# A hybrid mLSTM and stick-breaking layer on one core: every k turned by VectorE and DRAM, with the projections put in another order

## The chip, the core and the metric

The kernel runs on one core of a Trainium2 chip. A core has TensorE (PE: matmuls and their weight loads), VectorE (DVE), ScalarE (ACT), GpSimd (POOL) and SyncE (SP), which issues most DMAs. Each engine works through its own instructions in order and waits at semaphores for the others. The metric is the device time of one execution in microseconds. Names of engines and line numbers are those of the profile.

## What is computed

One layer on x of 512 tokens by 1024 channels, all in float32. The part that the change touches is stick-breaking attention: 8 heads of 128 channels, in two sets of four ("first" and "second" below), each with its own q, k, V and gate z, which are slices of one input projection.

```python
h = rmsnorm(x, norm_w)
proj = jnp.einsum('bsd,de->bse', h, w_in) + b_in
(mq, mk, mv, mi, mf, mo, mz, sq, sk, sv, sz, gates) = jnp.split(proj, split_at, axis=-1)
...
qs = rmsnorm(to_heads(sq, SB_HEADS), sb_q_norm_w)
ks_ = rmsnorm(to_heads(sk, SB_HEADS), sb_k_norm_w)
os_ = stick_breaking_attention(qs, ks_, to_heads(sv, SB_HEADS))
y_s = os_.transpose(0, 2, 1, 3).reshape(b_, s_, SB_WIDTH) * jax.nn.silu(sz)

g_m, g_s = jnp.split(jax.nn.sigmoid(gates), N_BRANCH, axis=-1)
merged = (g_m * jnp.einsum('bse,ed->bsd', y_m, w_proj_m)
          + g_s * jnp.einsum('bse,ed->bsd', y_s, w_proj_s))
x = x + jnp.einsum('bsd,de->bse', merged, w_out)
```

The other branch, an mLSTM (mq to mz, four heads of 256), runs behind the attention and is not changed.

## The kernel before

Every float32 product is made of three matmuls: both operands are split into a high and a low part (`split`, L99 to L101: ACT copies the high part, DVE subtracts it to get the low one), and high by high, high by low and low by high are added in PSUM (`mm3`, L95 to L97).

The projections are cut into units. A unit is one slice of weights (512 KB) with 24 matmuls of 512 columns. A loop over c runs them in order. In iteration c the kernel writes, in this order: the evacuation of unit c - 1 from PSUM; whatever was put down for c in `later` (`defer(n, fn)` puts it n units ahead, `at_unit(c, fn)` at a fixed place); the split of the weights of unit c + 2, and their loads up to unit c + 4 (`ahead`); the first half of unit c's matmuls; one step of each attention head that is running, and the first step of a head that begins; the second half of the matmuls. So each engine's order follows from the unit numbers. `by_dma` units have their low weights finished by a DMA that POOL issues and that adds (L127 to L129: two copies on ACT) and not by DVE.

Units of before: 0 to 3 first q; 4 to 7 half of the gates of the merge (GS), a filler while operands for the pairs are made; 8 to 21 and 22 to 35 two pairs; 36 to 39 first z; 40 to 43 second q; 44 to 47 second k; 48 to 51 second z; 52 to 55 half of GM, the other gates; then the mLSTM's. E is 36. A pair makes two projections together from 14 units of 12 matmuls each, by sums of weights (X, Y, V, Z) and of operands (`form`). The first pair is second V with the mLSTM's V, both parked in DRAM (`v_park`, L1060). The second is first V with first k. A pair's evacuation (`Pair.add`, L1040) adds the bias row on DVE; then a DMA from POOL (L1043) adds a part that ACT copied out earlier.

k and q come out with tokens on partitions. `norm` (L405) makes the sums of squares on ACT, four per 128 tokens; for k DVE scales the rows (L420). The scores need channels on partitions. `TURNED` lists which are turned without PE, two heads at a time (g 0 is heads 0 and 1, g 1 heads 2 and 3): `turn` (L432) transposes blocks of 32 by 32 on DVE into `ty`, `move` stores them to DRAM (`t_d`, four DMAs, L440), `back` loads them (`tz`, four DMAs, L445), and q's get their weight on DVE (L452). All of q is turned so, and k's g 1. k's g 0 is transposed by PE in the first step of its head (`head`, L482). That step also splits both operands (`qtt`, `ktt`). Step 1 makes the scores, steps 2 and 3 the products along the stick on DVE (L519 to L537); later steps turn the result through DRAM (`a_d`, `az`), split it (`ath`, `atl`) and multiply by V. First set's heads begin at units 37, 39, 42 and 44, second set's from unit 50 on. In a unit of `REST` no head steps.

Two pools of PSUM have four banks each: `dps` for units and a pair's bank "a", `aps` for attention and a pair's other banks. A unit of q or k by tokens needs four `dps` banks, two in each half of its first unit; a z or gate unit needs one.

Of the kernel before, what the change touches and what calls it, by code (L numbers as in the profile page):

```python
# [15 lines left out]
T = 512  # L16
# [22 lines left out]
def tile_hybrid_layer(  # L39
# [157 lines left out]
    later = {}  # L197
    now = [0]

    def by_plan(s, name, fn):  # L200
        if s:
            defer(1, fn)
        else:
            later.setdefault(E - 6, []).append(fn) if name == "q" else defer(2, fn)

    def defer(n, fn):
        later.setdefault(now[0] + n, []).append(fn)

# [150 lines left out]
    class SbSet:  # L359
# [5 lines left out]
            self.tz = {}  # L365
            self.count = {"q": 0, "k": 0, "v": 0}

        def z_group(self):
            def evac(ct, ps):
                sg = blk("tmp")  # L370
                b = bias(32 + 4 * self.s + ct)
                nc.scalar.activation(sg, ps, AF.Sigmoid, bias=b)
                t = blk("y", name="ys")
                nc.vector.scalar_tensor_tensor(t, ps, b, sg, op0=OP.add, op1=OP.mult)
                y_s[4 * self.s + ct] = t

            chan_group(w_in, C_SZ + 512 * self.s, 512, h_mov, evac)

# [19 lines left out]
        def norm(self, name, tb, t):  # L398
            self.raw[name][tb] = t
            ssq = tiny.tile([128, 4], F32, name="ssq", bufs=2)  # L400
            rr = tiny.tile([128, 8], F32, name="r" + name, bufs=8 if name == "q" else 4)
            r = rr[:, 0:4]
            junk = blk("om", BF, (128,), name="sqj")
            for h in range(4):
                nc.scalar.activation(junk, t[:, h * 128:(h + 1) * 128], AF.Square,  # L405
                                     accum_out=ssq[:, h:h + 1])
            rstd(r, ssq, 128, EPS)
            self.count[name] += 1
            last = self.count[name] == TB
            if name == "q":  # L410
                rn = rr[:, 4:8]
                nc.gpsimd.tensor_scalar(rn, r, -1.0, None, op0=OP.mult)
                self.r[tb] = (r, rn)
                if last:
                    by_plan(self.s, "q", lambda: self.turn(name, 0))
            else:
                def scale():
                    for h in range(4):
                        hs = slice(h * 128, (h + 1) * 128)
                        nc.vector.tensor_scalar(t[:, hs], t[:, hs], r[:, h:h + 1], None, op0=OP.mult)  # L420
                    if last:
                        done.add(("k", self.s))
                        by_plan(self.s, "k", lambda: self.turn(name, 1))
                defer(1, scale)

        def turn(self, name, g):

            ty = sp.tile([128, 8, TB, 32], F32, name="ty", tag="A", bufs=4)  # L430
            for tb in range(TB):
                nc.vector.transpose(ty[:, :, tb, :],  # L432
                                    self.raw[name][tb][:, 256 * g:256 * g + 256].rearrange("p (x j) -> p x j", j=32))

            def move():
                tz = blk("qk", F32, (2, 4, 128), name="tz")
                self.tz[name, g] = tz
                park = dp.tile([32, 2, 4, 4, 128], F32, name="t_d", tag="t_d", bufs=3)
                for a in range(4):
                    nc.sync.dma_start(park[:, :, :, a].rearrange("i h b x -> i (h b) x"),  # L440
                                      ty[32 * a:32 * a + 32].rearrange("i g n j -> i g (n j)"))

                def back():
                    for b in range(4):
                        nc.sync.dma_start(tz[32 * b:32 * b + 32].rearrange("i h a x -> i h (a x)"),  # L445
                                          park[:, :, b].rearrange("i h a x -> i h (a x)"))

                defer(2 if not self.s and name == "q" else 1, back)

            def weight():  # L450
                z = self.tz[name, g]
                nc.vector.tensor_scalar(z, z, qkw, None, op0=OP.mult)  # L452

            defer(1, move)
            if name == "q":
                defer(4 if self.s else 6, weight)
            if name == "q" and g == 0:
                defer(2, lambda: self.turn(name, 1))


        def v_parts(self, tb, t):
            vh = blk("vh", FR, (576,))[:, 0:512]
# [8 lines left out]
        def head(self, h):  # L471
            hs = slice(h * 128, (h + 1) * 128)
            tr = []
            for name in ("q", "k"):
                th, tl = own = two("qk", FR, name=name + "tt")
                if (name, self.s, h // 2) in TURNED:
                    tp = self.tz[name, h // 2][:, h % 2].rearrange("p a (i j) -> p i a j", j=32)
                    th, tl = [x.rearrange("p (i a j) -> p i a j", a=4, j=32) for x in own]
                else:
                    tp = att_ps()  # L480
                    for tb in range(TB):
                        nc.tensor.transpose(tp[:, tb * 128:(tb + 1) * 128], self.raw[name][tb][:, hs], ident)  # L482
                if name == "q" and not (name, self.s, h // 2) in TURNED:
                    nc.scalar.activation(th, tp, AF.Copy, scale=qkw)
                    nc.vector.scalar_tensor_tensor(tl, tp, qkw, th.bitcast(F32), op0=OP.mult, op1=OP.subtract)
                else:
                    split(tp, th, tl)
                tr.append(own)
            yield
            (qh, ql), (kh, kl) = tr  # L490
# [214 lines left out]
    class MPair:  # L705
# [11 lines left out]

            chan_group(w_in, C_MO + 512 * self.p, 512, h_mov, evac)

        def z_group(self):  # L720
            def evac(ct, ps):
                sg = blk("tmp")
                b = bias(24 + 4 * self.p + ct)
# [365 lines left out]
    for i in range(2):  # L1089
        at_unit(3, form_sum, 3, i)  # L1090

    for tb in range(TB):
# [480 lines left out]
```

## Time and profile before

| | us |
|---|---|
| median of 3 runs | 681.86 |
| the runs | 681.48, 681.86, 686.51 |
| the profiled execution | 686.68 |
| its span | 685.0 |
| DVE, busy | 497.3 |
| ACT, busy | 372.5 |
| POOL, busy | 114.9 |

The profile is of one execution, which took 1.7 us more than its span. Sums on its rows are compared with 686.68 first, and with the median after that. Unit 36 begins at 137.17 us, unit 37 at 142.61, unit 38 at 154.55, unit 45 at 199.00 and unit 46 at 207.79; units 47 and 48 begin at 214.49 and 219.94, unit 49 at 226.65. Matmul ends are modelled, so starts are the better guide: unit 36's 24 matmuls begin 0.227 us apart.

### The profile page before, as it was taken

To read this page: it belongs to the slowest core of one execution; us is meant where nothing else is said; L and a number is where in the kernel's file an instruction comes from. 1 tells how busy PE (TensorE), PEld (TensorE's weight loads), DVE (VectorE), ACT (ScalarE), POOL (GpSimd) and SP (SyncE) were. 2 spreads that over 40 slices of the span, in tenths; PEclk is the share of its full clock that TensorE was granted. 3 is DMA by queue.
4 is the path that set the end of the run, shared out by engine and by line. 5 is a ranking of instruction groups with operands and counts; after the bars stand their busy time and mean duration, and the time that the engine had idled before them with its cause. 6 is when DMAs were issued, how large, how long until landed. Compare 5 with 4: busy or idle time off the path is not lost.

```text
span 685.0 us, 9337 instructions
## 1 busy us (share of the span) xinstructions
PE 673.8 (98%) x3114; PEld 561.4 (82%) x3114; DVE 497.3 (73%) x852; ACT 372.5 (54%) x702; POOL 114.9 (17%) x265
## 2 busy tenths in 40 slices
PE   7999999989999999999999999999999999999998
PEld 5888888868888888888888888888888888888886
DVE  6777778756759878978888654569973466467997
ACT  6576545447586665654654646344455854234451
POOL 4023121412263222310011001110000120001020
PEclk9999999989999999999999999999999999999999
DMA  7566793965989866847458631435344468967333
GB/s 251 141 229 170 245 239 101 212 189 121 262 210 247 241 165 199 225 123 201 100 117 185 150 104 57 134 106 148 100 136 122 125 219 260 272 187 161 116 84 102
DMA packets 134464, 115.65 MB, mean 169 GB/s; under 512 B 17370, under 2 KB 105844, under 8 KB 134416
## 3 DMA queue, kind: packets, MB, share of 16 engines
q1 hardware_dynamic: 129232, 101.82, 51.1%
q0 software_dynamic: 5040, 13.11, 10.8%
q8 instruction: 24, 0.39, 0.2%
q14 instruction: 24, 0.20, 0.1%
q10 hardware_dynamic: 144, 0.13, 0.1%
HBM read 83.00 MB, written 18.93 MB: 149 GB/s over the span
## 4 chain that ended last, share of the span: by engine, by line
PE 91%; DMA 2%; DVE 2%; ACT 2%; issue 1%; POOL 1%; SPq 1%; DVEq 0%; ACTq 0%; POOLq 0%
PE dps L95 23%; PE dps L97 22%; PE dps L96 22%; PE dps L971 5%; PE aps L971 4%; PE aps L96 3%; PE aps L97 3%; PE aps L95 3%; DMA stg<-in_w_in_dram 2%; PE dps L1446 1%; PE dps L1448 1%; PE dps L1447 1%; ACT sqj L405 1%; PE aps L853 1%; PE aps L855 1%
## 5 line engine op out<-in xcount | busy, mean ns | idle before, releaser
L95 PE MATMUL dps<-hh,wh 128*128 128x512 f32 x448 | 176.4, 394 | 0.0
L97 PE MATMUL dps<-hh,wl 128*128 128x512 f32 x448 | 175.5, 392 | 0.0
L96 PE MATMUL dps<-hl,wh 128*128 128x512 f32 x448 | 175.4, 392 | 0.0
L101 DVE TENSOR_TENSOR wl<-stg,wh 128x1024 fp32r<-128x1024 f32 x73 | 89.2, 1222 | 69.5 <-ACT wh L100 68.8
L100 ACT ACTIVATE wh<-stg 128x1024 fp32r<-128x1024 f32 x73 | 76.7, 1052 | 42.9 <-PE dps L96 22.5
L97 PEld LDWEIGHTS dps<-hh,wl 128*128 128x128 f32 x448 | 84.7, 189 | 18.2
L96 PEld LDWEIGHTS dps<-hl,wh 128*128 128x128 f32 x448 | 84.8, 189 | 17.0
L95 PEld LDWEIGHTS dps<-hh,wh 128*128 128x128 f32 x448 | 84.9, 189 | 16.8
L743 ACT ACTIVATE tmp<-acc 128x512 f32<-128x512 f32 x16 | 10.1, 633 | 52.9 <-DVE acc L740 52.9
L95 PE MATMUL dps<-wh,hh 128*128 128x512 f32 x96 | 37.5, 391 | 0.0
L97 PE MATMUL dps<-wh,hl 128*128 128x512 f32 x96 | 37.4, 390 | 0.0
L96 PE MATMUL dps<-wl,hh 128*128 128x512 f32 x96 | 37.4, 390 | 0.0
L740 DVE SCALAR_TENSOR_TENSOR acc<-tmp,vec,acc 128x511 f32<-128x511 f32 (+2 forms) x48 | 36.0, 750 | 1.7
L519 DVE TENSOR_TENSOR_SCAN om<-om 128x512 f32<-128x512 f32 (+3 forms) x32 | 26.1, 816 | 0.0
L95 PE MATMUL dps<-yh,wh 128*128 128x512 f32 x64 | 24.9, 389 | 0.0
L96 PE MATMUL dps<-yl,wh 128*128 128x512 f32 x64 | 24.9, 389 | 0.0
L97 PE MATMUL dps<-yh,wl 128*128 128x512 f32 x64 | 24.9, 389 | 0.0
L129 POOL DMA_DIRECT2D wl<-stg x11 | 9.8, 888 | 89.6 <-DVE gback L1177 45.9
L507 ACT ACTIVATE om<-aps,rq 128x512 f32<-128x512 f32 (+3 forms) x32 | 16.7, 523 | 14.3 <-PE aps L97 14.3
L863 ACT ACTIVATE hns<-aps,hst 128x256 f32<-128x256 f32 x16 | 7.6, 475 | 28.2 <-DVE hst L862 21.1
L509 POOL TENSOR_SCALAR_AFFINE_SELECT om<-om 128x128 f32<-128x128 f32 x32 | 14.5, 452 | 44.5 <-ACT om L507 44.3
L101 DVE TENSOR_TENSOR atl<-az,ath 128x384 fp32r<-128x384 f32 (+1 forms) x24 | 13.8, 603 | 10.4 <-ACT ath L100 6.1
(303 smaller groups left out, 1533.9 us busy)
## 6 DMA issues: line engine op xcount, KB each, us to landing
stg<-in_w_in_dram SPq DMA_DIRECT2D x71, 512.0 KB, 4.8
wl<-stg POOLq DMA_DIRECT2D x11, 512.0 KB, 5.7
a_d<-ay SPq DMA_DIRECT2D x8, 640.0 KB
az<-a_d SPq DMA_DIRECT2D x32, 160.0 KB, 4.5
stg<-in_w_proj_s_dram SPq DMA_DIRECT2D x8, 512.0 KB
B<-in_w_out_dram SPq DMA_DIRECT2D x8, 512.0 KB, 8.3
stg<-in_w_proj_m_dram SPq DMA_DIRECT2D x8, 512.0 KB, 3.7
dst<-u POOLq DMA_DIRECT2D x12, 256.0 KB, 4.8
```

Of the source, the lines that this page charges most:

```text
L95: nc.tensor.matmul(ps, ah, bh, start=first, stop=False)
L96: nc.tensor.matmul(ps, ah, bl, start=False, stop=False)
L97: nc.tensor.matmul(ps, al, bh, start=False, stop=last)
L100: nc.scalar.activation(hi, src, AF.Copy)
L101: nc.vector.tensor_tensor(lo, src, hi.bitcast(F32), op=OP.subtract)
L129: nc.gpsimd.dma_start(out=self.wl, in_=self.st, accum_op=OP.add)
L507: nc.scalar.activation(om[:, 0:n], zp, AF.Sigmoid, scale=rn[:, h:h + 1])
L509: nc.gpsimd.affine_select(out=om[:, ts], in_=om[:, ts], compare_op=OP.is_gt, fill=1.0, base=0, channel_multiplier=1, pattern=[[-1, 128]])
L519: nc.vector.tensor_tensor_scan(back, back, back, 1.0, op0=OP.mult, op1=OP.bypass)
L740: nc.vector.scalar_tensor_tensor(acc[:, j:], t[:, 0:T - j], cw(3 - j, ch), acc[:, j:], op0=OP.mult, op1=OP.add)
L743: nc.scalar.activation(t, acc, AF.Sigmoid)
L971: nc.tensor.matmul(pr.bank[key, tb], a, w[:, i, :], start=begin and n == 0, stop=end and n == 2, skip_group_check=again)
```

## The change

No arithmetic changes. In the order of units, the filler 4 to 7 is first z, its result parked in DRAM (`z_park`) and loaded back in units 39 to 42 (`y_back`). The pair of first V and first k comes first (8 to 21), the pair of second V and the mLSTM's V next (22 to 35). Second q is 36 to 39, second k 40 to 43, second z 44 to 47, the half of GS that was the filler 48 to 51. The rest stays where it was.

All of k is turned by DVE and DRAM; `TURNED`, `by_plan` and PE's transposes go. For the first set q turns in units 9 and 13, k in 30 and 31 (`TURN`), and `tz` is loaded in units 33 and 37 for q, 34 and 38 for k (`TZ_BACK`). There `ty` lies in the buffers of tag qk, since the buffers A hold a pair's weights. For the second set, q and k turn one and two units behind their last norm. First heads begin at 36, 38, 41 and 44, and the first `REST` unit is 43 where it was 47. Weights finished by POOL's DMA are units 39 and 41 to 44, where they were 40 to 43 and 45 to 48.

```diff
-SB_START = [E + n for n in (1, 3, 6, 8, 14, 16, 18, 20)]
+SB_START = [E + n for n in (0, 2, 5, 8, 14, 16, 18, 20)]
-TURNED = {("q", 0, 0), ("q", 0, 1), ("q", 1, 0), ("q", 1, 1), ("k", 0, 1), ("k", 1, 1)}
-REST = {E + n for n in (11, 48)}
+TURN = {"q": (9, 13), "k": (30, 31)}
+TZ_BACK = {("q", 0): E - 3, ("q", 1): E + 1, ("k", 0): E - 2, ("k", 1): E + 2}
+REST = {E + n for n in (7, 48)}
...
-                t = blk("y", name="ys")
+                t = sg if dst is not None else blk("y", name="ys")
                 nc.vector.scalar_tensor_tensor(t, ps, b, sg, op0=OP.add, op1=OP.mult)
-                y_s[4 * self.s + ct] = t
+                if dst is None:
+                    y_s[4 * self.s + ct] = t
+                else:
+                    nc.sync.dma_start(dst[128 * ct:128 * ct + 128, :], t)
...
+        def turns(self, name):
+            for g in range(2):
+                if self.s:
+                    defer({"q": (1, 2), "k": (1, 2)}[name][g], lambda g=g: self.turn(name, g))
+                else:
+                    later.setdefault(TURN[name][g], []).append(lambda g=g: self.turn(name, g))
...
-                if (name, self.s, h // 2) in TURNED:
-                    tp = self.tz[name, h // 2][:, h % 2].rearrange("p a (i j) -> p i a j", j=32)
-                    th, tl = [x.rearrange("p (i a j) -> p i a j", a=4, j=32) for x in own]
-                else:
-                    tp = att_ps()
-                    for tb in range(TB):
-                        nc.tensor.transpose(tp[:, tb * 128:(tb + 1) * 128], self.raw[name][tb][:, hs], ident)
...
+                tp = self.tz[name, h // 2][:, h % 2].rearrange("p a (i j) -> p i a j", j=32)
+                th, tl = [x.rearrange("p (i a j) -> p i a j", a=4, j=32) for x in own]
+                split(tp, th, tl)
...
-        return lambda tb, t: defer(2 + tb % 2, lambda: sets[s].v_parts(tb, t))
+        return lambda tb, t: defer((2, 5)[tb % 2], lambda: sets[s].v_parts(tb, t))
...
-    chan_group(w_in, C_GS, 512, h_mov, park(gs_park, 48))
+    z_park = dp.tile([512, T], F32, name="z_park")
+    sets[0].z_group(z_park)
+    Pair(C_SV, C_SK, to_parts(0), to_norm(0, "k"))
     Pair(C_SV + 512, C_MV, to_dram(0), to_dram(1))
-    Pair(C_SV, C_SK, to_parts(0), to_norm(0, "k"))
...
+    for ct in range(4):
+        at_unit(E + 3 + ct, y_back, ct)
...
-    sets[0].z_group()
     sets[1].qk_group("q", C_SQ)
     sets[1].qk_group("k", C_SK)
     sets[1].z_group()
+    chan_group(w_in, C_GS, 512, h_mov, park(gs_park, 48))
...
-    for un in units[n_proj - 3:] + [units[E + n] for n in (4, 5, 6, 7, 9, 10, 11, 12)]:
+    for un in units[n_proj - 3:] + [units[E + n] for n in (3, 5, 6, 7, 8)]:
```

Line numbers of the changed kernel differ a little (L97 is L98 there, L374 is L369, L420 is L418, L432 is L435, L440 is L441, L445 is L448, L452 is L451, L1040 is L1030, L1060 is L1050, and a split's low part is L102). The order of instructions at three places follows.

SP before, from the first store of turned q (unit 31) to the loads for second q; `stg` is a slice of weights, `i_d` and `f_d` hold the mLSTM's gates:

```order
L440 DMA t_d<-ty 256x1x128 x4
L120 DMA stg<-in_w_in_dram 128x8x128
L445 DMA tz<-t_d 32x2x512 x4
L440 DMA t_d<-ty 256x1x128 x4
L120 DMA stg<-in_w_in_dram 128x8x128 x2
L633 DMA i_d<-g_1323 4x512
L634 DMA f_d<-g_1323 4x512
L445 DMA tz<-t_d 32x2x512 x4
```

SP in the changed kernel, from the same place:

```order
L441 DMA t_d<-ty 256x1x128 x8
L121 DMA stg<-in_w_in_dram 128x2x512
L448 DMA tz<-t_d 32x2x512 x4
L121 DMA stg<-in_w_in_dram 128x2x512
L448 DMA tz<-t_d 32x2x512 x4
L1050 DMA v_park<-dst 128x512 x2
L121 DMA stg<-in_w_in_dram 128x2x512
L623 DMA i_d<-g_1390 4x512
L624 DMA f_d<-g_1390 4x512
```

The loads for units 36, 37 and 38 are the first three of `stg` in both; two stores of V now stand ahead of the third, and both loads of `tz` ahead of `i_d`.

DVE before, units 34 to 37, from the low weights of unit 36 on (`dst` is a pair's result, here first V and k; `dst<-dst,rk` scales k):

```order
L101 TENSOR_TENSOR wl<-stg,wh 128x1024
L631 SCALAR_TENSOR_TENSOR g_1323<-aps,gbias,g_1321 36x512
L420 TENSOR_SCALAR dst<-dst,rk 128x128 x8
L101 TENSOR_TENSOR wl<-stg,wh 128x1024
L1040 TENSOR_TENSOR dst<-prow,dps 128x512 x2
L452 TENSOR_SCALAR tz<-tz,qkw 128x1024
L101 TENSOR_TENSOR wl<-stg,wh 128x1024
L374 SCALAR_TENSOR_TENSOR ys<-dps,bvec,tmp 128x512
L420 TENSOR_SCALAR dst<-dst,rk 128x128 x8
```

DVE in the changed kernel, from the same place:

```order
L102 TENSOR_TENSOR wl<-stg,wh 128x1024
L621 SCALAR_TENSOR_TENSOR g_1390<-aps,gbias,g_1388 36x512
L451 TENSOR_SCALAR tz<-tz,qkw 128x1024
L102 TENSOR_TENSOR wl<-stg,wh 128x1024
L1030 TENSOR_TENSOR dst<-prow,dps 128x512 x2
L102 TENSOR_TENSOR wl<-stg,wh 128x1024
L102 TENSOR_TENSOR qtt<-tz,qtt 128x512
L102 TENSOR_TENSOR ktt<-tz,ktt 128x512
```

k's scaling has left this place; the evacuation that frees two banks still stands behind the weights of unit 37, but unit 36 is now second q and needs those banks in its second half.

DVE before, units 48 to 50, between the evacuation of second k and the first head of the second set:

```order
L388 TENSOR_TENSOR kraw<-dps,brow 128x512 x4
L432 STREAM_TRANSPOSE ty<-qraw 128x8x32 x4
L101 TENSOR_TENSOR wl<-stg,wh 128x1024
L101 TENSOR_TENSOR atl<-az,ath 128x384
L519 SCALAR_TENSOR_TENSOR om<-om 128x256
```

DVE in the changed kernel, unit 46, whose second half steps the first set's last heads; unit 47 begins like it and then makes the `atl` that unit 48 multiplies:

```order
L369 SCALAR_TENSOR_TENSOR ys<-dps,bvec,tmp 128x512
L451 TENSOR_SCALAR tz<-tz,qkw 128x1024
L418 TENSOR_SCALAR kraw<-kraw,rk 128x128 x8
L102 TENSOR_TENSOR wl<-stg,wh 128x1024
L583 TENSOR_TENSOR ys<-aps,ys 128x512
L102 TENSOR_TENSOR atl<-az,ath 128x512
L102 TENSOR_TENSOR atl<-az,ath 128x384
L509 SCALAR_TENSOR_TENSOR om<-om 128x512
L510 TENSOR_TENSOR a_all<-a_all,om 128x512
L527 STREAM_TRANSPOSE ay<-a_all 128x4x32 x4
L509 SCALAR_TENSOR_TENSOR om<-om 128x128
L510 TENSOR_TENSOR a_all<-a_all,om 128x128
```

Second k's scalings and turns, and second z's products, now stand between the products of the first set's last heads; before they stood behind them.

More of the change, by code (lines that the diff above doesn't have):

```diff
@@ L366, in __init__, with z_group @@
             self.count = {"q": 0, "k": 0, "v": 0}
-        def z_group(self):
+        def z_group(self, dst=None):
             def evac(ct, ps):
@@ L414, in norm @@
                 if last:
-                    by_plan(self.s, "q", lambda: self.turn(name, 0))
+                    self.turns(name)
             else:
@@ L422, in scale @@
                         done.add(("k", self.s))
-                        by_plan(self.s, "k", lambda: self.turn(name, 1))
+                        self.turns(name)
                 defer(1, scale)
+        def turns(self, name):
[4 more added lines that the diff above has]
+                    later.setdefault(TURN[name][g], []).append(lambda g=g: self.turn(name, g))
         def turn(self, name, g):
-            ty = sp.tile([128, 8, TB, 32], F32, name="ty", tag="A", bufs=4)
+            ty = sp.tile([128, 8, TB, 32], F32, name="ty", tag=("qk", "A")[self.s],
+                         bufs=BUFS[("qk", "A")[self.s]])
             for tb in range(TB):
@@ L446, in back @@
                                           park[:, :, b].rearrange("i h a x -> i h (a x)"))
[L448 to L452, printed above, removed]
+                    if name == "q":
+                        defer(2, lambda: nc.vector.tensor_scalar(tz, tz, qkw, None, op0=OP.mult))
+                if self.s:
+                    defer(1, back)
+                else:
+                    later.setdefault(TZ_BACK[name, g], []).append(back)
             defer(1, move)
[L455 to L458, printed above, removed]
         def v_parts(self, tb, t):
@@ L718, in o_group, with z_group @@
             chan_group(w_in, C_MO + 512 * self.p, 512, h_mov, evac)
-        def z_group(self):
+        def z_group(self, dst=None):
             def evac(ct, ps):
```

19 lines of the change are left out of this document (6 added, 13 removed).

## The prediction

> **What bounds the kernel now.** I read the page's engine shares first, then the waits of PE, then PE's clock and busy time in the stretch that the waits point to. Columns of the page's row: busy us, share of the span, instructions; of a wait: us in total, times, longest; of a window: length, then each engine's busy us, granted clock, DMA share, GB/s.
>
> ```profile
> PE 673.8 (98%) x3114; PEld 561.4 (82%) x3114; DVE 497.3 (73%) x852; ACT 372.5 (54%) x702; POOL 114.9 (17%) x265
> ...
> PE aps L482 <- DVE dst L420: 2.7, 2, 2.4
> ...
> PE aps L96 <- DVE ktt L101: 0.4, 1, 0.4
> ...
> PE aps L482 <- DVE kraw L420: 0.2, 1, 0.2
> ...
> 137.17:142.61 5.44, 5.44 (x26) 4.50 (x24) 1.37 (x4) 1.98 (x7) 0.00 (x0) 1.00 0.76 217
> 142.61:154.55 11.94, 9.20 (x30) 6.84 (x28) 7.93 (x17) 5.79 (x17) 2.59 (x4) 0.72 0.55 168
> ```
>
> PE is the bound nearly everywhere. Time can be won only by giving PE less to do or by removing its few waits, and it is lost wherever another engine becomes late for PE. Unit 36 is the undisturbed price of a unit, 5.44 us. Unit 37, the next, lasts 11.94: PE is idle for 2.74 of it (11.94 less 9.20), and the granted clock is 0.72. The rows inside it say why:
>
> ```profile
> 140.57 1.06 ACT L100 ACTIVATE wh<-stg 128x1024 fp32r<-128x1024 f32 x1 [5.33 <-DMA stg<-in_w_in_dram]
> 142.81 1.28 DVE L1040 TENSOR_TENSOR dst<-prow,dps 128x512 f32<-128x512 f32 x2
> 147.61 1.65 DVE L420 TENSOR_SCALAR dst<-dst,rk 128x128 f32<-128x128 f32 x8
> 147.94 0.47 PE L482 MATMUL aps<-ident,dst 128*128 128x128 f32 x1 [2.43 <-DVE dst L420]
> 148.73 0.90 PE L482 MATMUL aps<-ident,dst 128*128 128x128 f32 x3 [0.31 <-DVE dst L420]
> 149.85 0.63 PE L96 MATMUL dps<-hl,wh 128*128 128x512 f32 x1
> ```
>
> ACT waits 5.33 us for a weight load, k's norms stand behind it on ACT, DVE scales k at 147.61, and PE's transposes of k wait for that. A matmul then takes 0.63 us. The clock stays down until unit 38 begins, so this one wait is paid nearly twice.
>
> **What the change removes.** The transposes of k on PE:
>
> ```profile
> L482 PE MATMUL aps<-ident,dst x8: 270/347/477, 147.9 to 165.0; 128*128 128x128 f32 x8
> L482 PE MATMUL aps<-ident,kraw x8: 270/272/330, 235.5 to 251.5; 128*128 128x128 f32 x8
> 164.84 0.44 PE aps L482 x4
> 251.31 0.44 PE aps L482 x4
> ```
>
> There are 16 of them, four to a head, and four take 0.44 on the chain of waits. In unit 37 everything over 5.44 goes: 6.50. The other three heads give 3 x 0.44 = 1.32, and the wait for kraw 0.16. That is 8.0 of the profiled execution. Of unit 37's 6.50, 3.32 (6.50 less 2.74 less 0.44) is the halved clock alone. The profiled execution took 686.68 and spans 685.0; the median of the runs is 681.86, and only one of the three (686.51) is like the profiled one. I take the two short runs to lack the halved clock; no trace of them is shown, so this is a choice. For the median the gain is then 8.0 - 3.3 = 4.7.
>
> **What it adds.** First, DVE and queue work. A turn of two heads costs DVE and SP this, and PE nothing:
>
> ```profile
> 118.62 1.42 DVE L432 STREAM_TRANSPOSE ty<-qraw 128x256 f32<-128x256 f32 x4
> 120.06 2.66 SPq L440 DMA_DIRECT2D t_d<-ty  x4
> 124.57 3.72 SPq L445 DMA_DIRECT2D tz<-t_d  x4
> 131.41 3.74 SPq L120 DMA_DIRECT2D stg<-in_w_in_dram  x2
> ```
>
> Two more turns are made (k's first halves): 2.84 of DVE and 16 issues on SP. The Trainium skill (VectorE: DVE Perf Modes, Rules for kernel authors) advises TensorE for a 128x128 transpose whose destination may be PSUM, so it speaks against this move. By the rows it is dear only where DVE is the late engine, since two heads cost PE 0.88 and DVE 1.42; there the sum would lose 1.42 and not gain 0.88, which is part of case C below. Elsewhere DVE's idle quarter covers it.
>
> First z as filler (units 4 to 7) adds an L374 of about 0.71 to each evacuation where a sigmoid and a store stood, and moves four of them out of units 37 to 40. DVE has room there, so nothing; if that cover went, the pair's weights would be late next.
>
> ```profile
> 40.00:60.00 20.00, 20.00 (x90) 16.57 (x89) 13.95 (x20) 16.83 (x47) 9.08 (x14) 1.00 0.58 188
> ```
>
> *k's norms in the first pair, units 20 and 22.* They stand on ACT ahead of the weights split for two units later. Before, the same order stood in unit 34:
>
> ```profile
> 128.10 0.39 PE L971 MATMUL dps<-wh,hh 128*128 128x512 f32 x1
> 128.74 0.31 ACT L405 ACTIVATE sqj<-dst 128x128 bf16<-128x128 f32 x1 [2.10 <-DMA dst<-u]
> 132.67 1.04 ACT L100 ACTIVATE wh<-stg 128x1024 fp32r<-128x1024 f32 x1
> 133.75 1.23 DVE L101 TENSOR_TENSOR wl<-stg,wh 128x1024 fp32r<-128x1024 f32 x1 [4.35 <-ACT wh L100]
> ```
>
> The weights were ready 6.88 after unit 34's first matmul (133.75 + 1.23 - 128.10). Two units of a pair last 5.44, so with the same waits PE stands 1.4 each time; with none it stands 0 (the gates' matmuls in unit 35 covered it before). I take 0.2 each, nearer to 0: 0.64 of the 6.88 was a wait for the sums to land, some more lay between the norms, and the stores of V that filled the queues of the first pair have left. Together 0.4, between 0 and 2.8.
>
> *Unit 36.* It was a z unit and needed one PSUM bank; now it is second q's first, and its second half needs the two banks that the pair's last evacuation (L1040) frees. That evacuation stands on DVE behind the weights of unit 37, which wait for their load. With before's times, the load ends at 140.57, the first bank is free at 142.81 + 0.64 = 143.45, 2.88 later, and PE wants it at 137.17 + 2.72 = 139.89: a wait of 3.6, the upper end. The lower is 0. SP issues the same 12 quarter-turns ahead of this load as before, and the second group of t_d is due one half unit, 2.72, earlier. The load at 137.85 gives a wait of 0.8, which I take.
>
> *Unit 37's scores* need k's tz halves, on ACT behind the weights of unit 38, whose load is now behind two v_park stores. Between 0 and the 2.74 of before; I take 0.5, near the low end, since no norm and no k scaling is left in that chain.
>
> *Units 44 to 48.* k's evacuation, two scalings and two turns, second z and weights that POOL's DMA finished before now meet set 0's last heads on DVE:
>
> ```profile
> 197.19:217.80 20.61, 20.16 (x96) 16.74 (x95) 17.18 (x40) 15.97 (x39) 11.41 (x27) 1.00 0.98 215
> 199.00:207.79 8.79, 8.34 (x40) 6.77 (x39) 5.80 (x14) 8.29 (x26) 6.30 (x16) 1.00 1.10 229
> 207.79:214.49 6.70, 6.70 (x35) 5.72 (x33) 6.53 (x16) 4.81 (x9) 3.30 (x11) 1.00 0.99 210
> 219.94:226.65 6.71, 6.71 (x32) 5.59 (x30) 5.34 (x11) 4.24 (x18) 2.44 (x4) 1.00 0.82 225
> 210.81 1.38 DVE L432 STREAM_TRANSPOSE ty<-qraw 128x256 f32<-128x256 f32 x4
> 217.80 1.20 DVE L101 TENSOR_TENSOR wl<-stg,wh 128x1024 fp32r<-128x1024 f32 x1
> 229.51 0.71 DVE L374 SCALAR_TENSOR_TENSOR ys<-dps,bvec,tmp 128x512 f32<-128x512 f32 x1
> 230.14 1.65 DVE L420 TENSOR_SCALAR kraw<-kraw,rk 128x128 f32<-128x128 f32 x8
> 234.41 0.74 DVE L452 TENSOR_SCALAR tz<-tz,qkw 128x1024 f32<-128x1024 f32 x1
> 206.25 0.56 DVE L101 TENSOR_TENSOR atl<-az,ath 128x384 fp32r<-128x384 f32 x1 [2.55 <-ACT ath L100]
> ```
>
> On before's clock: from unit 44's first atl at 197.19, DVE had 17.18 of work to the end of unit 46, with q's turn (1.38) in it. Now unit 45 adds 0.71 + 1.65 + 1.20, unit 46 0.71 + 0.74 + 1.65 + 1.20, unit 47 0.71 + 0.74 + 1.38 + 1.20 and the atl of 0.56 that PE needs in the middle of unit 48: 12.45. So that atl ends at 197.19 + 17.18 - 1.38 + 12.45 = 225.44. PE's units 45 to 47 hold 8.34, 6.70 and 6.71, so it is there at 199.00 + 21.75 + 2.72 = 223.47: a wait of 2.0. Unit 44's weights lose a second ACT copy (1.06, as L100), which lets DVE begin earlier: 0.9. I take 1.4, between the two. The ends: 0, and 2.0 + 3.43 = 5.4 if DVE idles as it did there (20.61 - 17.18). Apart from this, the 0.4 of wait for ktt in unit 45 stays.
>
> *The last turns of set 1* (k, units 47 to 50) follow this DVE stretch through SP; the score in unit 51 has about 1 us of room. Taken at 0, up to 2.0.
>
> New waits: 0.4 + 0.8 + 0.5 + 1.4 = 3.1. Against the profiled execution, 686.68 - 8.0 + 3.1 = 681.8; against the median, 681.86 - 4.7 + 3.1 = **680.3**.
>
> The waits are counted at full clock. The Trainium skill (TensorE: Matmul & The Clock Gate, HAM oscillation) lets the clock fall only for idle gaps over about 3.4 us. The rows here disagree: 2.43 and 0.31 were enough. The 0.4 in unit 45 was not. By the rule case C ends at 681.5; by the row it ends as computed.
>
> **The rivals.**
> A, the sum: 680.3, its own range 678 to 683.
> B, the new waits are all covered: 681.86 - 4.7 = 677.2. For it: DVE's idle quarter, and a DVE that is nearly free in units 36 and 37.
> C, DVE's overrun in units 44 to 48 reaches 2.6 us, and the clock halves as in unit 37: A less 1.4, plus 2.6 + 3.3, 684.8. For it: the 28.25 us of DVE work against 26.3 of PE time. Against it: one unit of slack that I may have counted too short.
> D, slower: SP's queue falls behind at units 32 to 38, where 0.5 MB of v_park and a second tz join. If 1.0 MB more comes ahead of unit 37's weights, at 236 GB/s they land 4.2 us after 140.57, and the bank wait is 3.6 + 4.2 = 7.8, with 3.3 for the clock and 2.3 of other waits: 690.6. It passes 1% from a landing at about 142.9 on. For it:
>
> ```profile
> 126.00:136.00 10.00, 10.00 (x45) 8.29 (x45) 5.03 (x11) 5.42 (x19) 4.48 (x7) 1.00 1.10 236
> SPq L1060 <- DMA dst<-u: 22.6, 6, 13.0
> ```
>
> the DMA engines are full there, and v_park has held SP for 13.0 us at a time. Against it: issue order, which puts the v_park behind that load.
>
> **How the numbers follow.** Chances: A 0.42, B 0.22, C 0.20, D 0.16. A measurement of this kernel tells about 1%, 6.8 us, from no change. The range, 676.0 to 687.5, takes in A, B, C and leaves D out. Faster than 675.0 needs more than B gives: 0.06. Slower than 688.7 is D: 0.16. The rest is 0.78.
>
> **What would show it.** Right: no L482 on PE, unit 37 near 6.6 us with the clock at 1.00, short PE waits for dst (L1040) in unit 36 and for atl in unit 48. A PE wait for atl over 2.4 with a clock under 1 after it is C; weights landing after 142.9 is D; no PE wait after 20 us is B. The prediction is wrong in its base if the short runs before already had no wait in unit 37.

## The result and the profile after

| | before | after |
|---|---|---|
| median of 8 runs, us | 681.72 | 687.38 |
| lowest to highest, us | 681.21 to 686.51 | 685.69 to 688.97 |
| profiled execution: time, span, us | 686.68, 685.0 | 685.69, 684.0 |

The change makes the kernel slower: ratio 1.0074, 95% interval 1.0051 to 1.0096, about 5 us (5.7 by the medians). Mind the two profiled executions: that of before is slower than each of its eight runs, that of after the fastest of its eight. Side by side they show a gain of 1 us that the runs do not have.

PE's row on the page after (busy us, share, instructions):

```profile
PE 670.9 (98%) x3098; PEld 557.9 (82%) x3098; DVE 503.0 (74%) x863; ACT 369.4 (54%) x699; POOL 119.0 (17%) x262
```

The 16 transposes are gone (3114 to 3098). PE's waits in the changed kernel (us in total, times, longest), without those of the kernel's start:

```profile
PE dps L97 <- DMA wl<-stg: 2.9, 1, 2.9
...
PE aps L97 <- DVE atl L102: 1.0, 1, 1.0
...
PE dps L961 <- DVE wl L102: 0.9, 1, 0.9
...
PE aps L97 <- DVE ktt L102: 0.7, 1, 0.7
PE aps L961 <- DVE wl L102: 0.4, 1, 0.4
PE dps L96 <- DVE dst L1030: 0.4, 1, 0.4
```

No wait for k's transposes is left; six others stand in its place. The windows of the units in which they lie (length, then busy us of each engine, granted clock, DMA share, GB/s) are those of units 22, 23, 24, 36, 37, 43 and 48:

```profile
94.75:97.73 2.98, 2.98 (x14) 2.18 (x12) 2.94 (x10) 2.71 (x14) 1.02 (x2) 1.00 0.02 3
97.73:101.69 3.96, 3.01 (x13) 2.18 (x12) 3.96 (x6) 2.90 (x5) 2.98 (x5) 1.00 0.09 19
101.69:105.16 3.47, 3.02 (x13) 2.18 (x12) 3.47 (x11) 2.07 (x3) 0.82 (x1) 1.00 1.03 191
138.72:144.94 6.22, 5.78 (x26) 4.43 (x25) 2.42 (x3) 1.06 (x1) 0.00 (x0) 1.00 1.04 319
144.94:152.81 7.87, 7.14 (x35) 5.68 (x33) 2.43 (x3) 5.78 (x9) 2.06 (x8) 1.00 1.06 349
...
184.22:192.87 8.65, 5.73 (x26) 4.43 (x24) 3.30 (x4) 3.97 (x16) 1.22 (x2) 1.00 1.01 262
220.31:227.75 7.44, 6.44 (x31) 5.19 (x30) 7.16 (x16) 1.64 (x2) 0.00 (x0) 1.00 0.42 95
```

Units 22 to 24 take 10.41 us where three units of a pair take 8.16 (2.72 each): 2.25 lost. Unit 36 loses 0.78 against 5.44; 0.44 of it is the wait for `dst`, the rest lies in the matmuls around it. Unit 43 stands for 2.92 (8.65 less 5.73 busy), unit 48 for 1.00. In units 23 and 24 DVE is busy from end to end; in unit 43 it is busy 3.30 of 8.65, so DVE cannot be the late engine there.

How the first loss comes about, from the trace of after, units 20 to 23, in order of time (start, duration, engine, line; in brackets the idle time before and what ended it). `sqj` are the squares of k's norms; the first and the last row of unit 20's sixteen stand here:

```profile
89.01 0.31 ACT L403 ACTIVATE sqj<-dst 128x128 bf16<-128x128 f32 x1 [1.16 <-DMA dst<-u]
...
92.66 0.19 ACT L403 ACTIVATION_READ_ACCUMULATOR sqj<-dst 128x1 f32 x1
92.75 2.00 ACT L101 ACTIVATE wh<-X 128x1024 fp32r<-128x1024 f32 x2
93.82 1.23 DVE L102 TENSOR_TENSOR wl<-X,wh 128x1024 fp32r<-128x1024 f32 x1 [3.52 <-ACT wh L101]
...
96.22 1.65 DVE L418 TENSOR_SCALAR dst<-dst,rk 128x128 f32<-128x128 f32 x8
97.79 1.22 DVE L102 TENSOR_TENSOR wl<-X,wh 128x1024 fp32r<-128x1024 f32 x1
...
99.06 0.50 PE L961 MATMUL dps<-wl,hh 128*128 128x512 f32 x1 [0.95 <-DVE wl L102]
```

Two blocks of squares hold ACT from 89.01 to 92.85, longer than the 2.72 us of such a unit. The weights wait behind them, DVE idles 3.52 us for `wh`, and then has weights, sums and k's scaling to do at once. PE gets `wl` 0.95 us late.

The second loss has to do with second q's norms. In the trace of before they began here, in unit 43:

```profile
191.42 0.33 ACT L405 ACTIVATE sqj<-qraw 128x128 bf16<-128x128 f32 x1
...
194.65 1.04 ACT L127 ACTIVATE wh<-stg 128x1024 fp32r<-128x1024 f32 x1
```

There too they stood ahead of weights, those of unit 46, but these were begun 13.1 us ahead of their unit (194.65 to 207.79). In the trace of after the norms have moved up with second q, and the weights behind them are begun 8.4 us ahead of unit 43 (175.81 to 184.22). Units 41 to 43:

```profile
172.59 0.31 ACT L403 ACTIVATE sqj<-qraw 128x128 bf16<-128x128 f32 x1
...
175.72 0.19 ACT L403 ACTIVATION_READ_ACCUMULATOR sqj<-qraw 128x1 f32 x1
175.81 1.04 ACT L128 ACTIVATE wh<-stg 128x1024 fp32r<-128x1024 f32 x1
176.76 1.04 ACT L129 ACTIVATE wl<-stg 128x1024 fp32r<-128x1024 f32 x1
...
178.22 0.23 POOL L410 TENSOR_SCALAR rq<-rq 128x4 f32<-128x4 f32 x1
178.78 0.94 POOL L130 DMA_DIRECT2D wl<-stg  x1 [0.32 <-issue]
...
187.52 0.50 PE L97 MATMUL dps<-wl,hh 128*128 128x512 f32 x1 [2.92 <-DMA wl<-stg]
```

ACT squares for 3.3 us (172.59 to 175.91) before it copies unit 43's weights. POOL, which has its own small steps of the same norms to do first (the last at 178.22), issues the DMA that finishes them at 178.78; unit 43 begins at 184.22 and gets them at 187.5. The wait's name says DMA, its cause may be ACT, POOL or the queue. The runs below go into that.

### The profile page after: what moved, and what is told of

Its sections match the earlier page's. It is cut to its first block, busy times and chain, and to the rows that moved or that the text cites. A ratio compares the mean times of both kernels' runs of the same rounds, so it can differ in the third digit from the quotient of the medians.

```text
span 684.0 us, 9345 instructions
## 1 busy us (share of the span) xinstructions
PE 670.9 (98%) x3098; PEld 557.9 (82%) x3098; DVE 503.0 (74%) x863; ACT 369.4 (54%) x699; POOL 119.0 (17%) x262
## 4 chain that ended last, share of the span: by engine, by line
PE 73%; DMA 6%; DVE 2%; POOL 1%; issue 1%; SPq 0%; ACT 0%; POOLq 0%; ACTq 0%
PE dps L96 21%; PE dps L97 21%; PE dps L98 21%; PE aps L97 3%; PE aps L98 3%; PE aps L96 3%; DMA tz<-t_d 2%; DMA wl<-stg 1%; DVE wl L102 1%; DMA a_d<-ay 1%; PE aps L843 1%; PE aps L845 1%; PE aps L844 1%; DMA v_park<-dst 1%; DMA dst<-u 1%
## 5 line engine op out<-in xcount | busy, mean ns | idle before, releaser
L98 PE MATMUL dps<-hh,wl 128*128 128x512 f32 x448 | 174.7, 390 | 0.0
L97 PE MATMUL dps<-hl,wh 128*128 128x512 f32 x448 | 174.6, 390 | 0.0
L102 DVE TENSOR_TENSOR wl<-stg,wh 128x1024 fp32r<-128x1024 f32 x76 | 92.9, 1222 | 80.8 <-ACT wh L101 74.7
L101 ACT ACTIVATE wh<-stg 128x1024 fp32r<-128x1024 f32 x76 | 79.9, 1053 | 51.1 <-PE dps L97 22.8
L98 PEld LDWEIGHTS dps<-hh,wl 128*128 128x128 f32 x448 | 84.1, 188 | 17.8
L97 PEld LDWEIGHTS dps<-hl,wh 128*128 128x128 f32 x448 | 84.2, 188 | 16.7
L97 PE MATMUL dps<-wl,hh 128*128 128x512 f32 x96 | 37.6, 392 | 2.9 <-DMA wl<-stg 2.9
L98 PE MATMUL dps<-wh,hl 128*128 128x512 f32 x96 | 37.5, 390 | 0.0
L499 POOL TENSOR_SCALAR_AFFINE_SELECT om<-om 128x128 f32<-128x128 f32 x32 | 19.6, 614 | 65.5 <-ACT om L497 65.5
L98 PE MATMUL dps<-yh,wl 128*128 128x512 f32 x64 | 24.9, 389 | 0.0
L97 PE MATMUL dps<-yl,wh 128*128 128x512 f32 x64 | 24.9, 389 | 0.0
L97 PEld LDWEIGHTS dps<-wl,hh 128*128 128x128 f32 x96 | 18.1, 188 | 6.7 <-DMA wl<-stg 3.3
L96 PEld LDWEIGHTS dps<-wh,hh 128*128 128x128 f32 x96 | 18.0, 188 | 4.7 <-DVE dst L1030 0.9
```

The costliest lines, as they stand in the source:

```text
L96: nc.tensor.matmul(ps, ah, bh, start=first, stop=False)
L97: nc.tensor.matmul(ps, ah, bl, start=False, stop=False)
L98: nc.tensor.matmul(ps, al, bh, start=False, stop=last)
L101: nc.scalar.activation(hi, src, AF.Copy)
L102: nc.vector.tensor_tensor(lo, src, hi.bitcast(F32), op=OP.subtract)
L499: nc.gpsimd.affine_select(out=om[:, ts], in_=om[:, ts], compare_op=OP.is_gt, fill=1.0, base=0, channel_multiplier=1, pattern=[[-1, 128]])
```

## The experiments

Every run was made beside runs of the kernel before on the same chip; ratios are against these (medians 682.12, 681.85, 682.42 and 682.05 us in the four groups). A ratio is taken over all the runs and differs from the quotient of the two medians by up to 0.002. Lines of the edited kernels are up to ten higher than those of the changed one.

**The kernel before, unchanged**, for a profile of its usual execution.

> The kernel before, unchanged, for a profile of its usual execution (the profiled one took 686.68 us, most runs 681.2 to 682.4, so about 5.0 are missing in a usual one). The prediction's choice: a usual run only lacks the halved clock (3.32), so unit 37 still lasts about 8.6 us with a PE wait for dst (L420) near 2.7 us, and 1.6 us are missing elsewhere. Theory now: the wait itself is missing; unit 37 lasts 7.0 us or less, PE waits for dst at L482 for under 1 us, the clock stays at 1.00. Rival: unit 37 is as in the profiled run, 11.9 us, and the 5 us are missing at the start (PE idles 2.9 us in units -1 and 0) or elsewhere.

It took 681.45 us, span 679.7. Unit 37 in the windows, and its rows in the trace:

```profile
142.05:149.42 7.37, 6.36 (x29) 4.85 (x28) 6.01 (x14) 4.01 (x7) 1.46 (x3) 1.00 0.62 179
```

```profile
138.09 1.06 ACT L100 ACTIVATE wh<-stg 128x1024 fp32r<-128x1024 f32 x1 [3.41 <-DMA stg<-in_w_in_dram]
...
145.15 1.65 DVE L420 TENSOR_SCALAR dst<-dst,rk 128x128 f32<-128x128 f32 x8
...
145.48 0.33 PE L482 MATMUL aps<-ident,dst 128*128 128x128 f32 x1 [0.55 <-DVE dst L420]
146.26 0.55 PE L482 MATMUL aps<-ident,dst 128*128 128x128 f32 x3 [0.46 <-DVE dst L420]
```

The theory holds in the main, though the unit is 0.4 us longer than its "7.0 us or less" and the two waits sum to 1.01. ACT waits 3.41 us for the weight load and not 5.33, PE waits 0.55 and 0.46 and not 2.43 and 0.31, and the clock stays at 1.00. Unit 37 lasts 7.37, not 11.94 and not the 8.62 that the prediction had chosen. So 4.57 of the 5.3 us between the two executions are there, 1.73 of them wait and 2.84 clock (9.20 less 6.36 busy). Of the 31 runs of the second group, 28 took 680.4 to 683.3 us and three 684.4 to 686.6 (in the third group six of 23 are above 684), so most runs are of this kind. Against this profile the changed one is not 1.0 us ahead but 4.3 behind (684.0 to 679.7).

**Unit 43's weights split by ACT and DVE.**

```diff
-    for un in units[n_proj - 3:] + [units[E + n] for n in (3, 5, 6, 7, 8)]:
+    for un in units[n_proj - 3:] + [units[E + n] for n in (3, 5, 6, 8)]:
```

> The changed kernel, with the weights of unit 43 split by ACT and DVE again and not finished by POOL's DMA. Theory: the 2.9 us that PE waited in unit 43 for wl by DMA go, together with the clock that some runs lose behind it (about 1.5); DVE idles 3.2 us in that stretch and takes the 1.2 us for nothing: 687.4 - 2.9 to 4.4 = 683.0 to 684.5 us, unit 43 lasts 5.4 to 6.0. Rival: DVE is the late engine there, so the wait only changes its name (atl, wl by DVE, or the scores' ktt in units 44 to 48) and the time stays at 686 to 688.

687.08 us, ratio 1.0080 (1.0060 to 1.0101): nothing won; the rival holds. The wait changed its name and place, as this run's trace shows in unit 42:

```profile
177.55 1.23 DVE L102 TENSOR_TENSOR wl<-stg,wh 128x1024 fp32r<-128x1024 f32 x1 [5.45 <-ACT wh L101]
178.69 0.68 DVE L509 TENSOR_TENSOR_SCAN om<-om 128x256 f32<-128x256 f32 x1
...
182.60 0.65 DVE L102 TENSOR_TENSOR qtt<-tz,qtt 128x512 fp32r<-128x512 f32 x1
...
183.91 0.50 PE L97 MATMUL aps<-ktt,qtt 128*128 128x512 f32 x1 [2.76 <-DVE ktt L102]
```

DVE now idles 5.45 us for ACT's `wh`, which stands behind the same squares; the scans and the next head's q and k queue behind it on DVE, which works almost without a gap from 177.55 until `ktt` is done. The rival had DVE late because it was overloaded. It is late because it waits for ACT. So the DMA is not the cause of the wait, and "DVE idles 3.2 us in that stretch" was no reason that an instruction put on it would be free.

**k's norms in the first pair one block at a time.**

```diff
-        return lambda tb, t: defer(2, lambda: sets[s].norm(name, tb, t))
+        return lambda tb, t: defer((2, 5)[tb % 2], lambda: sets[s].norm(name, tb, t))
```

> The changed kernel, with the two blocks of k's norms in the first pair no longer together in units 20 and 22 but apart, in units 20, 23, 22 and 25. Theory: 3.5 us of squares on ACT in one half unit of 2.72 us make the weights of units 23 and 24 late; with 1.75 us in a half unit they are in time, units 22 to 24 take 8.16 us again and not 10.42: 687.4 - 2.3 = 685.1 us. Rival: the norms' sum is what counts and the delay moves to units 25 to 27, or turns of k (units 30 and 31) become late: 687 or more.

685.60 us, ratio 1.0050 (1.0030 to 1.0069), 1.8 us under the changed kernel's 687.38; the two intervals overlap, so the runs alone do not settle it (a pair of runs further down does). Units 22 and 23 are back at 2.72, unit 24 still takes 3.33 with 0.3 of wait. The theory holds but for that rest. The wait for `dst` in unit 36 is gone too, but it comes and goes: over all the traces of the changed kernel and its variants unit 36 takes from 5.44 to 6.49, so this is not put down to the edit.

**Both edits.**

> The changed kernel, with both edits (weights of unit 43 by ACT and DVE; k's norms in units 20, 23, 22, 25). Theory: the two savings add, as they lie 80 us apart on PE's line: 687.4 - 2.3 - 2.9 to 4.4 = 680.7 to 682.2 us, which is the time of the kernel before within 1 us; what is left over to a gain is in the waits of units 36, 37 and 48 (2.1 us). Rival: only one helps, or a new wait comes in units 44 to 48: 683 us or more.

686.62 us, ratio 1.0069 (1.0053 to 1.0084): the first edit adds nothing to the second, and the forecast of a sum fails. The windows of unit 42, first of the run with the first edit alone, then of this one:

```profile
178.04:187.91 9.87, 7.11 (x34) 5.68 (x33) 8.18 (x20) 4.20 (x7) 2.91 (x9) 1.00 1.02 256
```

```profile
176.02:187.42 11.40, 8.62 (x35) 6.98 (x33) 8.20 (x20) 4.38 (x8) 3.03 (x9) 0.85 1.02 263
```

PE stands 2.76 us in the one and 2.78 in the other. In the first the clock stays at 1.00, in the second it is 0.85, and the same unit's work takes 8.62 and not 7.11 us: 1.5 us that come with a wait in one execution and not in another. The Trainium skill (TensorE: Matmul & The Clock Gate, HAM oscillation) lets the clock fall for idle gaps over some 3.4 us; this trace disagrees, with 2.78.

**One part undone: the first half of second k turned by PE again**, 8 matmuls in two heads in place of one turn on DVE.

```diff
+                if (name, self.s, g) == ("k", 1, 0):
+                    continue
...
+                if (name, self.s, h // 2) == ("k", 1, 0):
+                    tp = att_ps()
+                    for tb in range(TB):
+                        nc.tensor.transpose(tp[:, tb * 128:(tb + 1) * 128], self.raw[name][tb][:, hs], ident)
```

> The changed kernel, with one part undone: k's first half of the second set is turned by TensorE again (8 matmuls in two heads, 0.44 us a head), and the turn by DVE of it (1.42 us, 8 issues on SP) falls away. Theory: the turn sat on DVE right ahead of the weights and the atl that PE waits for in unit 48 (1.0 us), so this wait goes, and 0.9 comes back on PE: 687.4 + 0.9 - 1.0 = 687.3 us, no difference that can be measured; the profile shows no wait for atl in unit 48. Rival: the turn is free on DVE and atl is late for another reason, so the wait stays and the time is 688.3 us. Other rival: the queue work of the turn costs more than the one wait, and the time is 686 or less.

687.42 us, ratio 1.0078 (1.0051 to 1.0105), as forecast. The wait for `atl` in unit 48 is gone. Waits for `ktt` add up to 2.0 us (0.7 before the edit), so the two effects that the theory sets against each other are not measured apart here.

**The order of ACT in unit 41: weights first, norms behind them.** Nothing is added or taken away. POOL's small steps of these norms move behind its DMA as well, since they wait for the squares.

```diff
-                else:
+                elif name == "q":
+                    behind.setdefault(now[0] + 1, []).append(lambda: self.norm(name, tb, t))
+                else:
...
         ahead(c)
+        for fn in behind.pop(c, []):
+            fn()
         units[c].mm(0)
```

> The changed kernel, with one order on ACT changed: in unit 41 the weights of unit 43 are split ahead of the two blocks of second q's norms (3.5 us of squares) and not behind them; unit 43's wl is still finished by POOL's DMA. Theory: the wait of 2.9 us in unit 43 comes from the norms that second q, moved up right behind the pairs, puts ahead of the weights on ACT; the DMA is then issued at 174 to 175 and not 178.8, lands in time, and 2.9 us go, with up to 1.5 more that some runs lose to the clock: 683.0 to 684.5 us. Rival: it comes from the DMA queue, which took 8.9 us here because 512-byte packets of the turns were ahead of it: the wait stays at 1.5 us or more, 686 us or more. Other rival: the norms, now later, delay POOL's and DVE's work for the heads, and a wait for ktt or atl comes in units 42 to 45.

683.45 us, ratio 1.0025 (1.0011 to 1.0039): 3.9 us won by the medians, 3.3 by the ratios, and the interval lies below that of the changed kernel. The trace of this run, and unit 43 in its windows:

```profile
174.56 1.07 ACT L128 ACTIVATE wh<-stg 128x1024 fp32r<-128x1024 f32 x1
175.50 1.07 ACT L129 ACTIVATE wl<-stg 128x1024 fp32r<-128x1024 f32 x1
...
176.87 0.87 POOL L130 DMA_DIRECT2D wl<-stg  x1 [0.27 <-ACT sqj L406]
```

```profile
186.19:191.63 5.44, 5.44 (x25) 4.51 (x24) 3.21 (x4) 3.03 (x12) 0.21 (x2) 1.00 1.06 263
```

The DMA is issued 9.3 us ahead of unit 43 (186.19 less 176.87) and not 5.4 (184.22 less 178.78), and the unit takes the undisturbed 5.44. A wait of 0.3 us for a DMA of weights appears in unit 44. The unit begins 2 us later here than in the trace of after, since in this execution the kernel's start took 0.6 more, units 22 to 24 0.9 (11.28 in all) and units 36 and 37 0.4; at 684.74 us it is one of this version's slower ones.

The DMA also lands sooner. Its time from issue to landing, first in after, then here:

```profile
DMA to landing us min/median/max: 8.7/8.7/8.7
```

```profile
DMA to landing us min/median/max: 4.9/4.9/4.9
```

Counted from the start of unit 41 (171.94 and 173.92), ACT's two copies end 3.2 us earlier than in after, POOL issues 3.9 earlier, and the DMA is there 7.7 earlier. In after SP had issued a load of weights and four loads of `az` (from 176.77 on) ahead of this DMA; here they come behind it (from 178.74 on). By these numbers the earlier issue or the quicker landing would each have been enough: 178.78 + 4.9 = 183.7, before unit 43 begins at 184.22, and 176.87 + 8.7 = 185.6, before it begins at 186.19. So the run shows that the place of second q's norms brings the wait about, mostly through ACT. That SP's loads are what makes the DMA slow is argued and was not tested. With no DMA for these weights, in the run that gave them to DVE, PE stood nearly as long (2.76 us).

**Both orders on ACT mended**, k's norms apart and weights ahead of second q's norms.

> The two edits that move squares on ACT together: k's norms of the first pair in units 20, 23, 22 and 25, and in unit 41 the weights of unit 43 ahead of second q's norms. Theory: 685.6 (with the first alone) - 2.9 to 4.4 = 681.2 to 682.7 us, the time of the kernel before. Rival: a new wait in units 42 to 45, 684 us or more.

680.93 us, ratio 0.9983 (0.9969 to 0.9996). The loss is gone whole, 0.3 us under the forecast. Against the run with weights first alone, on the same chip, k's norms apart are worth 2.5 us, and here the intervals do not meet.

**And unit 48's weights by POOL's DMA** (12 added to the list of `by_dma`), as before the change.

> The same, and the weights of unit 48 finished by POOL's DMA, as in the kernel before, which takes 1.2 us off DVE ahead of the atl that PE waits for in unit 48. Theory: that wait (0.8 to 1.0 us) goes: 680.4 to 681.9 us, and the change with its collisions on ACT and DVE taken away is worth 0.3 to 1.7 us at most against the kernel before. Rival: POOL's DMA lands late for unit 48, and the time is 682 or more.

680.05 us, ratio 0.9963 (0.9947 to 0.9979). PE's waits in this run, those at the kernel's start left out:

```profile
PE aps L97 <- DVE ktt L102: 0.9, 1, 0.9
PE dps L98 <- DMA wl<-stg: 0.4, 1, 0.4
PE aps L964 <- DVE wl L102: 0.3, 1, 0.3
```

The wait for `atl` is gone, as forecast, and the time is 0.35 under the forecast range. This version beats both kernels; the 0.9 us to the version above is within the intervals.

**The same with the first half of second k on PE**, and **the same with the first head's q and k ahead of unit 38's weights**, on another chip. The second moves the first head's start ahead of `ahead(c)` in unit 36 (two further lines keep that head from being started and stepped twice):

```diff
+        if c == E:
+            act.append(sets[0].head(0))
+            next(act[-1])
         ahead(c)
```

> The repaired kernel (k's norms of the first pair apart, weights of unit 43 ahead of second q's norms, unit 48's weights by POOL's DMA; 680.05 us), and the first half of k of the second set turned by TensorE again. Theory: in the changed kernel this undoing was worth nothing (687.42 against 687.38) only because the other waits moved with it; here nothing collides, so the two heads pay 2 x 0.44 = 0.88: 680.9 us, and the four heads of the whole change are worth 1.76. Rival: the turn of two heads on DVE, SP and DMA costs as much as it saves even here: 680.0 or less.

> The repaired kernel, and in unit 36 the split of the first head's q and k put ahead of unit 38's weights on ACT and DVE (they waited behind a weight load of 5.5 us for no reason of their own). Theory: the wait for ktt in unit 37 (0.9 us) goes and nothing else moves: 679.1 us. Rival: tz itself comes late from DRAM, then the weights of unit 38 are late as well and the time is 680 or more.

682.60 us, ratio 0.9999 (0.9982 to 1.0017), and 683.35 us, ratio 0.9995 (0.9973 to 1.0018). The first lies above both of its forecasts (680.9, and 680.0 or less), but could not be set against the 680.05 of another chip, hence the last two runs. In the second the wait in unit 37 went as foreseen, but the rest of the theory fails. The windows of units 37 and 45 in this run:

```profile
142.71:149.54 6.83, 6.83 (x35) 5.76 (x33) 1.23 (x1) 4.85 (x7) 2.01 (x8) 1.00 1.06 328
...
193.96:203.81 9.85, 8.35 (x41) 6.77 (x40) 9.57 (x24) 8.47 (x27) 7.17 (x11) 1.00 0.90 216
```

Unit 37 falls from 8.10 to 6.83, but PE stands 1.50 us for `ktt` in unit 45, where DVE is busy 9.57 of 9.85, and 0.75 for a DMA of weights in unit 42. PE is sooner where it will be held up anyway. Why the later waits grow past what was won was not traced further.

**The repaired kernel and its variant with second k on PE, side by side.**

> The repaired kernel (as in the run with unit 48's weights by POOL's DMA, 0.9963 of the kernel before) once more, so that it stands on one chip beside the next run. Theory: the gain is real, 0.994 to 0.998 of the kernel before, about 2.5 us. Rival: it belonged to the chip or to the hour, and the ratio is 1 within its interval, as the two later runs on another chip had it.

> The repaired kernel with the first half of k of the second set turned by TensorE, beside the run above on the same chip. Theory: 0.88 us slower than the repaired kernel (two heads of 0.44), a ratio to before 0.0013 higher. Rival: 2.5 us slower, as the two earlier runs on different chips had it, which needs a further wait. Other rival: no difference.

680.92 us, ratio 0.9981 (0.9967 to 0.9994), and 680.88 us, ratio 0.9985 (0.9968 to 1.0001). The repaired kernel's gain stands, at 0.2 to 0.4% by the two ratios (0.17 and 0.26% by the medians). Whether PE or DVE turns these two heads cannot be told from the times: the ratios differ by 0.0004, the forecast difference was 0.0013, and the intervals reach 0.0014 and 0.0017 to each side. The price on PE is in the traces all the same: units 50 and 52, in which these heads begin, take 6.68 and 7.23 us with the turn on DVE, 7.11 and 7.68 with PE, 0.88 in all as forecast; waits elsewhere that differ from one execution to the next hide it. The further wait of the 2.5 us rival does not show. By the Trainium skill (VectorE: DVE Perf Modes, Rules for kernel authors) PE is the place for such a transpose; these two runs speak neither for nor against it.

## Why the prediction was wrong

It forecast 680.3 us with the likeliest range 678 to 683; the time is 687.38, at the upper end of the wide range, and none of the cases A to D is what happened. Step by step:

| step | forecast, us | measured, us |
|---|---|---|
| unit 37 in a usual run before | 8.62 | 7.37 |
| taken away, in a usual run | 4.7 | 3.4 |
| k's norms in the first pair | 0.4 (0 to 2.8) | 2.25 |
| bank wait, unit 36 | 0.8 (0 to 3.6) | 0.78 |
| first scores, unit 37 | 0.5 (0 to 2.74) | 0.73 |
| second q's norms, unit 43 | no term | 2.92 |
| `atl`, unit 48 | 1.4 (0 to 5.4) | 1.00 |

- **The base** failed first: "I take the two short runs to lack the halved clock". They lack most of the wait as well. The gain in a usual run is 1.93 in unit 37 (7.37 less 5.44), with 1.32 and 0.16 taken as forecast: 3.4, not 4.7. The halved clock itself cost 2.84 and not 3.32. The step was marked as a choice; its other side, that the wait itself comes and goes, here with a weight load that lands 1.9 us sooner or later, was the true one.
- **k's norms** had the right cause and the wrong end of the range: "I take 0.2 each, nearer to 0". The bound worked out from the rows of unit 34, 1.4 for each, was close for the first pair of blocks (1.5 lost in units 22 and 23) and high for the second (0.75 in unit 24, of which 0.6 stays with the norms apart). The reasons for going low (a wait for the sums, the stores of V) did not touch the squares themselves, which keep ACT for 3.8 us in a unit of 2.72.
- **Second q's norms** were left out, and this is the largest miss. The part on units 44 to 48 counted DVE's work and took it as the late engine there. That second q's 3.3 us of squares move ahead of weights in units 40 and 41 was not counted at all, though the same kind of work was priced three paragraphs earlier; they stood ahead of weights before too, but with 13.1 us to the unit and not 8.4. The run with only this order changed won 3.9 us.
- **The small waits** (units 36, 37, 48) were right in place and cause, and their sizes are within 0.4 us. For unit 36 that is luck in part: other executions lost from 0 to 1.05 there. A wait of the length of case C's (2.6 us) did come, but in unit 43 and from ACT, and in the profiled execution it did not halve the clock.
- **Case D** did not occur: in after ACT began unit 37's weights at 139.07, 0.4 us behind the start of unit 36; D needed them to land 5.7 us behind it (142.9 less 137.17).

The sum with the measured terms is 681.86 - 3.4 + 7.7 = 686.2 us, against 685.69 in the profiled execution; from span to span it is 679.7 - 3.4 + 7.7 = 684.0, which is the span of after. The 0.4 of wait in unit 45 that was to stay is gone as well, so differences of that size cancel in this sum.

The median lies 1.7 above the profiled execution. In seven of the eight runs the mean granted clock was 0.994 to 0.998 (1.0 in the profiled one). A mean of 0.998 is half clock for 0.4% of 685 us, 2.7 us, which costs 1.4. That this goes with the wait in unit 43 was not seen in a profile of after itself, but the runs speak for it. Of the 12 runs of the two kernels that have this wait of 2.9 us (after, and k's norms apart) 10 show 0.998 or less (3 of 6 where it is 2.4, with half of second k on PE); of the 44 runs of the repaired kernel and its stages with weights first 5. The wait is not the only occasion: 23 of the 86 runs of before show it too, and in the trace of the repaired kernel with second k on PE on the other chip the clock is 0.62 from 10.00 to 14.50 us, long before unit 43.

So the change's own gain, the transposes and the waits that go with them, was small, 3.4 us by the rows. More than that was lost, most of it to squares that the new order put on ACT ahead of weights with too little time left for them. With these two places and unit 48 mended it is worth 0.2 to 0.4%; how much of that is the turns and how much the order of the units was not told apart.

## What to carry to other kernels

When a group of units is moved, price what its evacuation defers to every engine, in the units where that lands; an engine with half its time free is still late if 3.3 us of it stand ahead of the one instruction that others wait for. A wait named after a DMA or after DVE is read back through the queue until an engine is found that was busy rather than waiting: moving the work to another messenger gained nothing, changing the order at the source gained 3.9 us. And profile a usual run before the sum is made: here 5 us of the profile before belonged to that execution alone.

## What the hardware showed

- Equal waits of PE, 2.76 and 2.78 us in the same unit, left the clock at 1.00 in one execution and lowered it to 0.85 over the unit in another, at 1.5 us. In the profiled execution before, 2.43 of wait and the 0.31 behind it came with 2.84 lost in clock. The stretches of low clock, first in the profiled execution before, then in the run with both first edits:

```profile
147.80:154.50 6.70, 6.25 (x16) 4.85 (x17) 3.79 (x11) 0.75 (x2) 0.00 (x0) 0.50 0.52 157
```

```profile
181.85:185.15 3.30, 3.25 (x11) 2.86 (x12) 2.64 (x8) 1.91 (x4) 0.84 (x4) 0.50 1.11 300
```

Each begins as the wait ends (at 147.94, with the 0.31 still to come, and at 181.91), the clock is 1.00 on either side, and the first is twice as long. A wait of this length is thus worth its length, or about one and a half to two times that, by the execution.

- In the execution of before in which unit 37's weights landed 1.9 us sooner (ACT waited 3.41 and not 5.33), unit 37 was 4.57 us shorter.
- The DMA that finishes unit 43's weights (512 KB) landed 8.7 us after its issue in after (178.78 to 187.5) and 4.9 us after it in the run with weights first; the one for unit 44 took 9.1 and 9.5. So issued 5.4 us ahead it was late, and 9.3 us ahead it was not.
